# Output projection as seven half-size products, with half of the transposes under the last one

## The chip, the core and the metric

The kernel runs on one core of a Trainium2 chip. The time is what the device needs for one execution, in microseconds (us); lower is better. Work is done by TensorE (PE in the profile; its weight loads are PEld), VectorE (DVE), ScalarE (ACT), GpSimd (POOL) and by DMA transfers, which are issued from the queues of SyncE (SP), ScalarE and GpSimd. Each engine runs its own instructions in order and waits at semaphores for the others.

## The reference

One decoder block with x of 512 x 2048 (sequence S = 512, width D = 2048), in float32:

```python
h = rms_norm(x, norm1_g)
z = h @ w_in
o_rw = rwkv7_mix(token_shift(z[..., :3520], rw_mu), ...)
o_att = swa_attention(q, k, v, q_norm_g, k_norm_g, attn_sinks)
p_rw = o_rw @ w_branch[:1024]
p_att = o_att @ w_branch[1024:]
x = x + (sigmoid(zg_rw) * p_rw + sigmoid(zg_att) * p_att) @ w_out
h2 = rms_norm(x, norm2_g)
u = h2 @ w_up
c = causal_conv3(u) + conv_b
val, gate = split(c)
x = x + (silu(gate) * val) @ w_down
```

w_in is 2048 x 9152, w_out 2048 x 2048, w_up 2048 x 11264 (D_FF = 5632, twice), w_down 5632 x 2048.

## The kernel before, in words

Every product of float32 data is made of three matmuls: each operand is rounded to a reduced format (`hi`, on ScalarE) and the remainder is kept too (`lo`, on VectorE); hi x hi, lo x hi and hi x lo are added up in PSUM. A large product is therefore bound by its matmuls and fed by loads and splits.

The work runs in five stages.

- *First stage*, to about 1291 us. x is normalised and transposed, z is computed in 72 tiles of 128 columns, and attention, RWKV heads and gates are computed between them. `load_w` (L228 and following) loads 256 KB of weights into one of four `raw` buffers on SP's queue and splits it into `whi` and `wlo`. Each third call also runs one job of `sums_along`: a copy of 512 KB from DRAM to DRAM on SP's queue (L219) and an adding DMA of the same size on GpSimd's queue (L220). The 88 jobs make four sums of quarters of w_down, s1 to s4, for 11 blocks. The stage ends with the two branch outputs, o_at and o_rw, loaded back from DRAM and split.
- *Branch product*, L778 to L791, to about 1466 us. For each of 16 tiles m of 128 output columns, both halves of w_branch are multiplied (768 matmuls of 128 x 512), the gates are applied, and the merged tile is split into `mhi` and `mlo`, in SBUF (L790, L791).
- *Output projection*, L803 to L821, to about 1640 us. For four blocks of 512 columns, 16 tiles k and four row tiles, three matmuls each: 768 matmuls of 128 x 512. w_out comes through `load_w`, 64 loads of 256 KB. After each column block the sum is added to x1 (L818), squared for the norm (L820) and stored to `x1_d` (L821, GpSimd's queue).
- *Up projection*, to about 2573 us. x1 is normalised (a reduction L823, the small operations L187 to L194, the scaling L829/L831) and transposed by 64 TensorE transposes (L980), which are evacuated by ScalarE and VectorE (L990, L988). The transposed x1 is kept as four quarters q11, q12, q21, q22 (rows of weights by halves of the sequence). Then w_up is applied in 44 blocks, each as seven products of half size in place of eight, P1, P2, P7, P6, P5, Q4, P3, with 24 matmuls x 7 of 128 x 256 in a block (L899). Seven right-hand factors are made from the quarters and split (L994, L995): b11, b21, b22 are quarters, t1 = q11 - q12, t3 = q22 - q12, t2 = -t1 - q22 and t4 = -t2 - q21 are differences (L1049, L1050, L1056, L1057). Weights of a block are split on L885/L886. A list `steps` near L998 gives the order of products of neighbouring blocks; loads are issued from `queue`.
- *Down projection*, L1108 to the end. Also seven half-size products, each over 11 chunks; a chunk loads 256 KB of the right factor from DRAM (`h_d`, L1113), splits it (L1115, L1116), loads two weights or sums of 512 KB (L1119), splits them (L1121, L1122), and runs 24 matmuls of 128 x 512 (L1129). A product has 264 matmuls. The seven factors of h are made by VectorE in the up projection and written to DRAM by ScalarE's queue.

The seven-product form multiplies a 2 x 2 arrangement of blocks by seven block products, not eight. What it needs beside them are sums of weight quarters (s1 to s4 in DRAM) and differences of the right-hand quarters.

SBUF and PSUM come from pools; a tile that takes the place of an earlier one waits for the last reader of that place. Instructions on SP's queue run in order, so that a load that waits holds up all loads behind it. The planner that turns the program into five queues keeps the data's order and otherwise may move an instruction of one engine ahead of another; `pin` keeps some in program order.

Of the kernel before, what the change touches and what calls it, by code (L numbers as in the profile page):

```python
# [18 lines left out]
P = 128  # L19
# [115 lines left out]
def block_kernel(ctx: ExitStack, tc: tile.TileContext, d: Dims, a: dict, out: bass.AP):  # L135
# [11 lines left out]
    NB = NF // 4  # L147
    DH = d.D // 2
    h_d = [dram.tile([7, P, 2, S // 2], F32, name=f"h_d{j}") for j in range(NB)]
    sum_d = {n: [dram.tile([2, P, DH], F32, name=f"{n}_d{j}") for j in range(NB)] for n in ("s1", "s2", "s3", "s4")}  # L150

# [50 lines left out]
    def quarter(i, j, c):  # L202
        return a["w_dn"][i, j, 2 * c : 2 * c + 2]

    jobs = []
    for kinds in (
        (("s1", (1, 0), (1, 1)), ("s3", (0, 0), (1, 0))),
        (("s2", "s1", (0, 0)),),
        (("s4", "s2", (0, 1)),),
    ):  # L210
        jobs += [(k, c, q) for c in range(NB) for q in range(2) for k in kinds]
    pin = tc.keep_in_program_order

    def sums_along():

        if jobs:
            (n, first, second), c, q = jobs.pop(0)
            at = lambda src: (sum_d[src][c] if isinstance(src, str) else quarter(*src, c))[q]
            pin(sync.dma_start(sum_d[n][c][q], at(first), max_dma_last_dim=4096))  # L219
            pool.dma_start(sum_d[n][c][q], at(second), accum_op=ALU.add, max_dma_last_dim=4096)  # L220
# [7 lines left out]
    def load_w(src):  # L228
# [9 lines left out]
        if wp["n"] % 3 == 0:  # L238
            sums_along()
# [35 lines left out]
    if True:  # L275
# [466 lines left out]
        ohi = by_k(big(xbp, "ohi", "h2"), NP + NQ)  # L742
        olo = by_k(big(xbp, "olo", "l2"), NP + NQ)
        tbs = ExitStack()
        tb = tbs.enter_context(tc.tile_pool(name="tb", bufs=2, reuse_waits="tile"))
        srcs = []
        for nm, src, n in (("a", o_at_d, NQ), ("r", o_rw_d, NP)):
            at = 0 if nm == "r" else NP
            hi, lo = ohi[:, at : at + n], olo[:, at : at + n]
            for i in range(n):  # L750
                o = tb.tile([P, 2, S], F32, name="oin", tag="gin")[:, 0]
                act.dma_start(o, src[i * P : (i + 1) * P])
                split(hi[:, i], lo[:, i], o)
                if i % 2:
                    emit_gate()
            srcs.insert(0, (hi, lo, n))
        while gates:
            emit_gate()
    pa.close()
# [5 lines left out]
    wbc = ExitStack()  # L765
    open_weights(wbc, 4, 4)
    mhi = by_k(big(big1, "mhi", "h1"))
    mlo = by_k(big(big1, "mlo", "l1"))
    with ExitStack() as pbb:
        accp = pbb.enter_context(tc.tile_pool(name="accB", bufs=4, space=PSUM, reuse_waits="tile"))  # L770
        XC = NT * d.D // NK
        for m in range(NK):
            g = tb.tile([P, 2, S], F32, name="gin", tag="gin")
            for i in range(2):
                act.dma_start(g[:, i], gate_d[(i * NK + m) * P : (i * NK + m + 1) * P])
            r0 = 0
            for i, (hi, lo, n) in enumerate(srcs):
                acc = accp.tile([P, S], F32, name="acc", tag="acc")  # L778
                wb = a["w_b"][m].rearrange("p (k c) -> p k c", c=P)[:, r0 : r0 + n]
                project(acc, wb, hi, lo)  # L780
                if i == 0:
                    w = min(XC, d.D)
                    for e in range(m * XC, (m + 1) * XC, w):
                        t, c0 = divmod(e, d.D)
                        with tc.issue_after(wp["last"].ins):
                            sync.dma_start(x1[:, t, c0 : c0 + w], xd[t * P : (t + 1) * P, c0 : c0 + w])
                r0 += n
                dve.scalar_tensor_tensor(g[:, i], g[:, i], 1.0, acc, op0=ALU.add, op1=ALU.mult)
            dve.tensor_tensor(g[:, 0], g[:, 0], g[:, 1], op=ALU.add)
            act.activation(mhi[:, m], g[:, 0], AF.Copy, scale=0.5)  # L790
            dve.scalar_tensor_tensor(mlo[:, m], g[:, 0], 0.5, mhi[:, m].bitcast(F32), op0=ALU.mult, op1=ALU.subtract)  # L791
    tbs.close()
    xbs.close()


    KH = NK // 2
    TH = S // 2
    pc = ExitStack()
    tcp = pc.enter_context(tc.tile_pool(name="tcp", bufs=1, reuse_waits="tile"))
    cps = ExitStack()  # L800
    accp = cps.enter_context(tc.tile_pool(name="accC", bufs=8, space=PSUM, reuse_waits="tile"))
    CW = min(S, d.D)
    NCC = d.D // CW  # L803
    ssp = tcp.tile([P, NT, NCC], F32, name="ssp")
    for cc in range(NCC):
        cs = slice(cc * CW, (cc + 1) * CW)
        accs = [accp.tile([P, S], F32, name="acc", tag="acc") for _ in range(NT)]
        for k in range(NK):
            whi, wlo = load_w(a["w_out"][k * P : (k + 1) * P, cc * CW : (cc + 1) * CW].rearrange("(k p) c -> p k c", p=P))
            whi, wlo = whi[:, 0], wlo[:, 0]  # L810
            for t in range(NT):
# [36 lines left out]
    def raw_tile(nm="raw", n=6):  # L848
        return rwp.tile([P, WC], F32, name=nm, tag=nm, bufs=n)
# [366 lines left out]
```

## Time and profile before

| | |
|---|---|
| median of 3 runs | 3008.12 us (3006.22 to 3010.33) |
| profiled execution, its own time | 3003.21 us |
| its span | 3001.4 us |
| matmuls and transposes on TensorE | 18890 |
| busy: TensorE / VectorE / ScalarE / GpSimd | 2911.7 / 1904.8 / 1292.7 / 172.8 us |
| mean granted TensorE clock | 0.99 |

The profile is of one execution. Its busy times say how long each engine worked; the windows view cuts the span into stretches and gives the same per stretch, with the granted TensorE clock (1.00 is full) and the share of the 16 DMA engines in use. A row of the groups view reads: line, engine, operation, output <- inputs, shape, count | busy us, mean ns of one | idle time of that engine before them, and what ended it. A matmul's own duration there is longer than the distance between two matmuls, since they overlap; the pace is read from a long run of them in the chain of waits (start, length, what, count). A row of the timeline is start, length, engine, line, operation, and in brackets the idle time before it and what ended it.

### The profile page before, as it was taken

What the parts mean: (1) busy time and instruction counts of PE and PEld (TensorE: products, weight loads), DVE (VectorE), ACT (ScalarE), POOL (GpSimd) and SP (SyncE); (2) the same over time, 40 slices, a digit from 0 to 9 for tenths busy, and PEclk for the clock granted to TensorE, in tenths of its full rate; (3) what the DMA queues carried; (4) which work ended last, traced back from release to release, by engine and by line L of the source; (5) the groups of instructions that cost most, each with busy time, mean ns of one, the idle gap of its engine ahead of it and who ended that gap; (6) DMA issues with size and microseconds to landing.
All of it is one profiled execution on the core that took longest, in us unless ns stands there. A gap on an engine that the chain in (4) does not pass through costs nothing.

```text
span 3001.4 us, 48098 instructions
## 1 busy us (share of the span) xinstructions
PE 2911.7 (97%) x18890; PEld 2486.0 (83%) x18890; DVE 1904.8 (63%) x3183; ACT 1292.7 (43%) x2129; POOL 172.8 (6%) x224
## 2 busy tenths in 40 slices
PE   6899999999999999999999799999999999999999
PEld 5677777777777777788887799999999999888887
DVE  4456566666666766434333877777777787665555
ACT  4234344344334434422232545555555555444444
POOL 0000100000000000000000000000000000000000
PEclk9999999999999999999999999999999999999999
DMA  7654756656656656645444577778777777777775
GB/s 208 172 137 121 192 125 171 157 130 168 159 137 161 162 139 162 207 140 169 126 126 120 153 188 203 201 207 208 208 206 207 205 201 206 289 239 245 255 256 190
DMA packets 210582, 544.44 MB, mean 181 GB/s; under 512 B 23009, under 2 KB 43185, under 8 KB 209329
## 3 DMA queue, kind: packets, MB, share of 16 engines
q1 hardware_dynamic: 143136, 385.00, 42.3%
q0 software_dynamic: 28416, 104.87, 18.4%
q10 hardware_dynamic: 38800, 51.48, 5.1%
q8 instruction: 148, 2.42, 0.3%
q14 instruction: 82, 0.66, 0.1%
HBM read 498.95 MB, written 133.54 MB: 211 GB/s over the span
## 4 chain that ended last, share of the span: by engine, by line
PE 88%; DVE 4%; DMA 3%; ACT 2%; issue 1%; ACTq 0%; DVEq 0%; SPq 0%
PE X L899 16%; PE acc L251 10%; PE acc L252 10%; PE acc L250 9%; PE Y L899 8%; PE X L1129 8%; PE Y L1129 6%; PE Z L899 4%; PE acc L815 2%; PE acc L816 2%; PE acc L814 2%; DMA rsb<-rsd 1%; DMA rsd<-rsT 1%; PE mi L428 1%; PE bulk L674 1%
## 5 line engine op out<-in xcount | busy, mean ns | idle before, releaser
L235 ACT ACTIVATE whi<-raw 128x512 fp32r<-128x512 f32 x416 | 261.6, 630 | 587.5 <-PE acc L251 376.1
L236 DVE TENSOR_TENSOR wlo<-raw,whi 128x512 fp32r<-128x512 f32 x416 | 285.5, 689 | 325.3 <-ACT whi L235 316.5
L250 PE MATMUL acc<-xhi,whi 128*128 128x512 f32 x1152 | 468.6, 407 | 4.6 <-ACT whi L235 2.7
L252 PE MATMUL acc<-xhi,wlo 128*128 128x512 f32 x1152 | 471.6, 409 | 0.6 <-DVE wlo L236 0.5
L251 PE MATMUL acc<-xlo,whi 128*128 128x512 f32 x1152 | 469.4, 408 | 0.0
L1122 DVE TENSOR_TENSOR wlo<-raw,whi 128x1024 fp32r<-128x1024 f32 x154 | 188.4, 1225 | 153.9 <-ACT whi L1121 152.4
L899 PE MATMUL Y<-t,whi 128*128 128x256 f32 x1408 | 259.7, 285 | 11.3 <-ACT whi L885 6.7
L899 PE MATMUL X<-t,whi 128*128 128x256 f32 x1408 | 259.5, 285 | 5.0 <-ACT u L909 5.0
L886 DVE TENSOR_TENSOR wlo<-raw,whi 128x1024 fp32r<-128x1024 f32 x176 | 215.2, 1223 | 73.1 <-ACT whi L885 72.8
L899 PE MATMUL X<-b,whi 128*128 128x256 f32 x1408 | 258.0, 283 | 2.5 <-DVE b L995 1.6
L250 PEld LDWEIGHTS acc<-xhi,whi 128*128 128x128 f32 x1152 | 219.1, 190 | 46.9 <-issue 3.7
L252 PEld LDWEIGHTS acc<-xhi,wlo 128*128 128x128 f32 x1152 | 218.9, 190 | 43.3 <-issue 2.9
L251 PEld LDWEIGHTS acc<-xlo,whi 128*128 128x128 f32 x1152 | 219.3, 190 | 42.2 <-issue 1.2
L1121 ACT ACTIVATE whi<-raw 128x1024 fp32r<-128x1024 f32 x154 | 163.0, 1060 | 204.6 <-PE X L1129 102.9
L885 ACT ACTIVATE whi<-a 128x1024 fp32r<-128x1024 f32 x132 | 139.4, 1056 | 216.4 <-DVE a L880 210.1
L899 PEld LDWEIGHTS Y<-t,whi 128*128 128x128 f32 x1408 | 221.2, 193 | 12.2 <-ACT whi L885 6.9
L899 PEld LDWEIGHTS X<-t,whi 128*128 128x128 f32 x1408 | 221.4, 194 | 5.2 <-ACT u L909 5.2
L899 PEld LDWEIGHTS X<-b,whi 128*128 128x128 f32 x1408 | 219.8, 192 | 3.0 <-DVE b L995 1.8
L886 DVE TENSOR_TENSOR wlo<-a,whi 128x1024 fp32r<-128x1024 f32 x132 | 161.8, 1226 | 75.4 <-ACT whi L885 74.7
L899 PE MATMUL X<-t,wlo 128*128 128x256 f32 x704 | 200.6, 285 | 0.5 <-DVE wlo L886 0.5
L899 PE MATMUL Y<-t,wlo 128*128 128x256 f32 x704 | 200.2, 284 | 0.6 <-DVE wlo L886 0.6
L899 PE MATMUL X<-b,wlo 128*128 128x256 f32 x704 | 199.4, 283 | 1.1 <-DVE wlo L886 1.1
(326 smaller groups left out, 6037.5 us busy)
## 6 DMA issues: line engine op xcount, KB each, us to landing
raw<-in_w_up_dram SPq DMA_DIRECT2D x176, 512.0 KB
raw<-in_w_z_dram SPq DMA_DIRECT2D x288, 256.0 KB
s_d<-in_w_dn_dram POOLq DMA_DIRECT2D x88, 512.0 KB, 5.9
raw<-in_w_up_dram POOLq DMA_DIRECT2D x88, 512.0 KB, 9.2
raw<-s_d SPq DMA_DIRECT2D x88, 512.0 KB
raw<-in_w_dn_dram SPq DMA_DIRECT2D x66, 512.0 KB
s_d<-in_w_dn_dram SPq DMA_DIRECT2D x44, 512.0 KB
s_d<-s_d SPq DMA_DIRECT2D x44, 512.0 KB
```

The costliest lines, as they stand in the source:

```text
L235: act.activation(hi, raw, AF.Copy)
L236: dve.tensor_tensor(lo, raw, hi.bitcast(F32), op=ALU.subtract)
L250: pe.matmul(acc, whi[:, j], xhi[:, k], start=first, stop=False)
L251: pe.matmul(acc, whi[:, j], xlo[:, k], start=False, stop=False)
L252: pe.matmul(acc, wlo[:, j], xhi[:, k], start=False, stop=last)
L814: pe.matmul(dst, mhi[:, k, ts], whi, start=k == 0, stop=False)
L885: pin(act.activation(hi, t, AF.Copy))
L886: pin(dve.tensor_tensor(lo, t, hi.bitcast(F32), op=ALU.subtract))
L899: pin(pe.matmul(ps, l[:, k], r[:, k], start=start and k + i == 0, stop=last and i == 2, skip_group_check=True))
L1121: act.activation(whi, wr, AF.Copy)
L1122: dve.tensor_tensor(wlo, wr, whi.bitcast(F32), op=ALU.subtract)
L1129: pe.matmul(dst, l[:, q, ts], r[:, es], start=fst and j == 0, stop=lst and j == 2, skip_group_check=True)
```

## The change

The output projection takes the form of the down projection. w_out is arranged as quarters (`w_o`) like w_down, and both share the code: `PRODUCTS`, `steps_of` (one chunk: one 256 KB load of a right factor, its split, two loads of 512 KB, their splits, 24 matmuls) and `taken_out` (four additions into x). For w_out there are four chunks, 96 matmuls in a product, 672 in all. The sums s1 to s4 are made for w_out too: 120 jobs, those for w_out first, one at every second `load_w`.

The branch product takes the tiles m in pairs (attention half of m and m+1, then RWKV half of m and m+1). A merged pair is not split any more: VectorE makes t1, t3, t2, t4 from it, and ScalarE's queue stores three pieces (128, 256 and 512 KB) to `right_d["o"]` in DRAM. The RWKV half of the branch input is loaded by two DMAs of 1 MB on GpSimd's queue, and its split goes to the memory of the first stage's right-hand side. The weight tiles of the projection (`hlD`, `rawD`, `hhlC`) are opened where the branch product's right-hand side (`rhi`, `rlo`) and the other tiles of that stage were.

Under the last of the seven products the first half of the rows (row tiles 0 and 1) is normalised, transposed after two and after three of the four chunks (16 transposes each, by `transposed`), and split to b11 and b21. The other half is normalised and transposed between the first steps of the up projection. The accumulator Y of the up projection comes from its own pool, `upy`, and the first steps are reordered.

```diff
@@ sums
+    for w in ("o", "dn"):
+        for kinds in (
+            (("s1", (1, 0), (1, 1)), ("s3", (0, 0), (1, 0))),
+            (("s2", "s1", (0, 0)),),
+            (("s4", "s2", (0, 1)),),
+        ):
+            jobs += [(w, k, c, q) for c in range(NB[w]) for q in range(2) for k in kinds]
...
-        if wp["n"] % 3 == 0:
+        if wp["n"] % 2 == 0:
             sums_along()
@@ end of the first stage
+        for i in range(2):
+            pool.dma_start(rin[i], o_rw_d.rearrange("(i n p) s -> i p n s", i=2, p=P)[i])
         while gates:
             emit_gate()
+        rhi = by_k(big(big1, "rhi", "h1"), NP)
+        rlo = by_k(big(big1, "rlo", "l1"), NP)
+        for i in range(NP):
+            split(rhi[:, i], rlo[:, i], rin[2 * i // NP][:, i % (NP // 2)])
@@ branch product
-            act.activation(mhi[:, m], g[:, 0], AF.Copy, scale=0.5)
-            dve.scalar_tensor_tensor(mlo[:, m], g[:, 0], 0.5, mhi[:, m].bitcast(F32), op0=ALU.mult, op1=ALU.subtract)
+                if m % 2:
+                    tq = mp.tile([P, 4, TH], F32, name="tq", tag="tq")
+                    factors(tq, *mt, 0)
+                    factors(tq, *mt, 1)
+                    store_factors("o", m // 2, *mt, tq)
@@ output projection
-        for k in range(NK):
-            whi, wlo = load_w(a["w_out"][k * P : (k + 1) * P, cc * CW : (cc + 1) * CW].rearrange("(k p) c -> p k c", p=P))
...
+    def steps_of(w, i, acc, c, pl):
+
+        nm, start, src, right, _ = PRODUCTS[i]
+        hr = pl.tile([P, 2, TH], F32, name="hraw", tag="hraw")
+        sync.dma_start(hr, right_d[w][c][RIGHT_AT[right]])
+        hhi, hlo = (pl.tile([P, 2, TH], F32R, name=f"h{e}", tag=f"h{e}") for e in ("hi", "lo"))
+        act.activation(hhi, hr, AF.Copy)
+        dve.tensor_tensor(hlo, hr, hhi.bitcast(F32), op=ALU.subtract)
+        for q in range(2):
+            wr = raw_tile()
+            sync.dma_start(wr, quarter(w, src, c)[q])
+            whi, wlo = (hlp.tile([P, WC], F32R, name=f"w{e}", tag=f"w{e}") for e in ("hi", "lo"))
+            act.activation(whi, wr, AF.Copy)
+            dve.tensor_tensor(wlo, wr, whi.bitcast(F32), op=ALU.subtract)
...
+    def row_done(i, t, cc, cs):
+        sq = hp.tile([P, S], F32, name="sqc", tag="sqc", bufs=2)
+        act.activation(sq, x1[:, t, cs], AF.Square, accum_out=ssp[:, t, cc : cc + 1])
+        (act if i == 6 else pool).dma_start(x1_d[t * P : (t + 1) * P, cs], x1[:, t, cs])
...
+            if last:
+                yx.close()
+                tps = tpx.enter_context(tc.tile_pool(name="tpD", bufs=4, space=PSUM, side="right", reuse_waits="tile"))
+                normalise(0)
+            for c in range(NB["o"]):
+                steps_of("o", i, acc[nm], c, hp)
+                if last and c == NB["o"] - 3:
+                    transposed(tps, 0, 0, q11)
+                    split_q("b11", q11)
+                if last and c == NB["o"] - 2:
+                    transposed(tps, 1, 0, q21)
+                    split_q("b21", q21)
+            taken_out(i, acc[nm], x1, 0.5, row_done)
@@ first steps of the up projection
-    transposed(0, (q11, q12))
-    split_q("b11", q11)
-    transposed(1, (q21, q22))
...
+    run(0)
+    normalise(1)
+    run(1)
+    run(2)
+    transposed(tps, 0, 1, q12)
+    dve.tensor_tensor(q11, q11, q12, op=ALU.subtract)
+    run(3)
+    transposed(tps, 1, 1, q22)
...
+    dve.tensor_tensor(q12, q22, q12, op=ALU.subtract)
+    split_q("t3", q12)
+    run(4)
+    split_q("t1", q11)
+    dve.scalar_tensor_tensor(q11, q11, -1.0, q22, op0=ALU.mult, op1=ALU.subtract)
+    run(5)
+    split_q("t2", q11)
```

395 lines of the change are left out of this document (187 added, 208 removed).

## The prediction

> **What bounds the kernel now.** I read the page first: the busy times, the slices, and the chain of work that ended last.
>
> ```profile
> span 3001.4 us, 48098 instructions
> PE 2911.7 (97%) x18890; PEld 2486.0 (83%) x18890; DVE 1904.8 (63%) x3183; ACT 1292.7 (43%) x2129; POOL 172.8 (6%) x224
> PE   6899999999999999999999799999999999999999
> DMA  7654756656656656645444577778777777777775
> ...
> PE 88%; DVE 4%; DMA 3%; ACT 2%; issue 1%; ACTq 0%; DVEq 0%; SPq 0%
> ```
>
> TensorE is busy in 97% of the span and carries 88% of the chain, so the time is the number of matmuls times their pace, plus the places where TensorE waits. The slices show one such place after the start, a 7 in the 23rd slice, about 1650 us. The windows by stage say which stage that is (columns: window, its length, busy time of PE, PEld, DVE, ACT, POOL, granted clock, DMA share, GB/s):
>
> ```profile
> 0.00:100.00 100.00, 71.97 (x317) 56.94 (x317) 42.69 (x121) 38.28 (x70) 6.05 (x11) 0.93 0.75 211
> 900.00:1100.00 200.00, 198.34 (x1487) 151.02 (x1486) 134.76 (x297) 85.29 (x173) 12.62 (x16) 1.00 0.60 150
> 1291.00:1466.00 175.00, 175.00 (x774) 144.95 (x773) 80.55 (x124) 49.69 (x79) 0.00 (x0) 1.00 0.56 161
> 1466.00:1640.00 174.00, 174.00 (x769) 144.15 (x768) 52.84 (x79) 47.35 (x89) 7.07 (x13) 1.00 0.40 106
> 1640.00:1707.00 67.00, 47.76 (x330) 44.92 (x329) 57.00 (x68) 37.01 (x48) 7.40 (x11) 0.85 0.64 173
> 1707.00:2573.00 866.00, 856.55 (x7105) 855.14 (x7104) 675.99 (x809) 440.71 (x598) 71.87 (x82) 1.00 0.77 202
> 2573.00:3001.00 428.00, 423.05 (x1877) 349.63 (x1875) 254.98 (x267) 203.72 (x233) 2.17 (x4) 1.00 0.75 250
> ```
>
> The branch product (1291 to 1466) and the output projection (1466 to 1640) have no idle time at all. The seam from the projection to the up projection (1640 to 1707) has 19 us idle at a clock of 0.85. The other stages lose little.
>
> **What the matmuls that go are worth.** Groups of matmuls and the chain give the pace:
>
> ```profile
> L814 PE MATMUL acc<-whi,mhi 128*128 128x512 f32 x256 | 99.6, 389 | 0.0
> ...
> 2637.70 59.84 PE Y L1129 x264
> ```
>
> The projection is three such groups of 256, 768 matmuls; seven products of 4 chunks x 2 x 2 x 2 x 3 = 96 make 672. The chain's piece from the down projection is the same product form, 264 matmuls in 59.84 us, 0.2267 us each and without a gap. So the 96 that go are worth 96 x 0.2267 = 21.8 us. That form needs 8 weight loads of 512 KB and 4 of 256 KB for 96 matmuls, what the down projection needs too, where 250 GB/s were moved while TensorE stayed busy. I therefore cost the loads at nothing inside the projection; DMA and the splits below hide behind the matmuls.
>
> ```profile
> L1121 ACT ACTIVATE whi<-raw 128x1024 fp32r<-128x1024 f32 x154 | 163.0, 1060 | 204.6 <-PE X L1129 102.9
> L1122 DVE TENSOR_TENSOR wlo<-raw,whi 128x1024 fp32r<-128x1024 f32 x154 | 188.4, 1225 | 153.9 <-ACT whi L1121 152.4
> L1116 DVE TENSOR_TENSOR hlo<-hraw,hhi 128x512 fp32r<-128x512 f32 x77 | 52.7, 685 | 13.0 <-ACT hhi L1115 13.0
> L788 DVE SCALAR_TENSOR_TENSOR gin<-gin,acc 128x512 f32<-128x512 f32 x32 | 22.0, 688 | 49.8 <-PE acc L252 49.8
> ```
>
> Per product VectorE does 8 x 1.23 + 4 x 0.69 and four additions of 0.69, 15.3 us under 21.8 us of matmuls; without that cover they would cost themselves. In the branch product the split of the merged rows goes and factors and their stores come. VectorE was busy 80.6 of 175 us there; also nothing. Ahead of it, the eight splits of the RWKV half now wait for the last matmul of the first stage, whose memory they take: 8 x 0.69 = 5.5 us under the attention half's 48 matmuls of 0.2267, 10.9 us, for which weights are loaded already; nothing, or 5.5 without them.
>
> **Seam one, branch product to projection, is new.** Before, nothing waited there. Now the weight tiles of the projection lie in memory that the branch product's right-hand side has just left, so SP's first weight load waits for the last matmul of the branch product. SP's queue takes loads in order: everything behind it waits too. After that matmul come issue, landing, ScalarE's rounding, VectorE's remainder. The nearest rows are those at 1640 us, where SP also loads after a stage:
>
> ```profile
> 1640.49 0.33 SPq L870 DMA_DIRECT2D a<-in_w_up_dram  x1
> ...
> 1701.89 6.37 DMA a<-in_w_up_dram
> ...
> raw<-in_w_up_dram POOLq DMA_DIRECT2D x88, 512.0 KB, 9.2
> x_d<-x POOLq DMA_DIRECT2D x16, 256.0 KB, 3.8
> ```
>
> A 512 KB landing is between the 3.8 of a half-size transfer and 9.2 of a POOL load in a busy queue; I take the 6.4 of the load on SP's queue in the chain, since up to three 256 KB factor loads are ahead of ours. With 1.06 for the first rounding TensorE is idle 0.3 + 6.4 + 1.1 = 7.8 us; the third matmul wants the remainder, most of whose 1.2 us passes under two slow matmuls: 0.5 more, 8.3. VectorE's last merge and factors, some 2.6 us, pass under the landing. An idle stretch of that kind costs again through the clock, as the seam at 1675 us shows:
>
> ```profile
> 1675.04 0.58 PE L899 MATMUL Y<-t,whi 128*128 128x256 f32 x1 [6.66 <-ACT whi L885]
> ...
> 1675.04:1681.42 6.38, 4.95 (x19) 4.36 (x20) 6.34 (x5) 0.41 (x2) 0.00 (x0) 0.50 0.28 82
> 1794.75:1800.90 6.15, 5.96 (x26) 5.66 (x27) 4.95 (x6) 2.60 (x4) 0.00 (x0) 0.50 0.31 91
> ```
>
> After 6.7 us of idle time the granted clock was 0.50 for 6.4 us, and after another idle time for 6.2 us, so half of that, 3.2 us, is lost. Seam one: 8.3 + 3.2 = 11.5 us, between 5.7 + 3.2 = 8.9 with 3.8 and 11.1 + 3.2 = 14.3 with 9.2. Below nothing there is no room, since no idle time was there before.
>
> The Trainium skill, "TensorE: Matmul & The Clock Gate", Part 1 on the HAM clock gate, gives a re-warming of about 3.4 us at half rate after an idle window, which would cost 1.7 and not 3.2 us. By it the seam is 10.0 and the whole sum 1.5 us lower. The trace's two rows of over 6 us at 0.50 do not agree, and the sum goes by them.
>
> **The transposes under the last product.** Thirty-two of 64 transposes move from seam two to the last product:
>
> ```profile
> 1645.43 6.36 PE L980 MATMUL ps_t<-ident,x 128*128 128x128 f32 x32 [4.97 <-DVE x L831]
> 1652.81 3.71 PE L980 MATMUL ps_t<-ident,x 128*128 128x128 f32 x32 [1.02 <-DVE x L988]
> 1642.03 0.17 DVE L823 TENSOR_REDUCE ss<-ssp 128x4 f32<-128x16 f32 x1 [0.85 <-ACT sqc L820]
> ...
> 1644.42 0.16 DVE L194 SCALAR_TENSOR_TENSOR rq<-rq,rq 128x4 f32<-128x4 f32 x1
> 1644.62 2.74 DVE L831 TENSOR_SCALAR x<-x,rq 128x1024 f32<-128x1024 f32 x4
> ```
>
> At the full clock 32 take 3.7 us, and they stand between matmuls: +3.5. Their input needs four VectorE additions (2.8), squares, the chain from 1642.03 to 1644.6 with four splits between its steps on VectorE, and two scalings of 0.76 that also wait for the stores of x1: some 10 to 12 us after the product begins, while TensorE comes to them after two of four chunks, 48 x 0.2267 = 10.9 us. 0 to 2 us of wait; I take 1. Together +4.5.
>
> **Seam two, projection to up projection.** Before, the first eleven steps of the up projection and the 64 transposes run from the last matmul of the projection to here:
>
> ```profile
> 1640.07 0.39 PE L816 MATMUL acc<-wlo,mhi 128*128 128x512 f32 x1
> ...
> 1707.12 0.40 PE L899 MATMUL X<-t,whi 128*128 128x256 f32 x2
> ...
> 1639.18 1.41 ACT sqc L820 x4
> ...
> 1688.82 2.87 PE X L899 x24
> ...
> 1665.35 2.28 DVE L1049 TENSOR_TENSOR x<-x 128x2048 f32<-128x2048 f32 x1
> 1688.76 2.29 DVE L995 TENSOR_TENSOR t<-x,t 128x2048 fp32r<-128x2048 f32 x1
> ```
>
> From 1640.3 to 1707.1 are 66.8 us. Of them 11 x 24 matmuls of 0.12 (2.87 us for 24 in the chain) are 31.7 and the transposes some 7 at the full clock; 28 are stalls. With the change three steps can run at once, on the factors that were split under the last product. But the first weight's rounding stands behind four squares (1.41 for two with their accumulator reads, so 2.8) and the stores on ScalarE, and the remainder stands behind the second normalisation's small operations: first full pace at about +7.7 us. Three steps of 2.9 and the transposes bring it to +24. The next factor then needs, on VectorE alone and in a row, a difference, a remainder, evacuations, two differences and two more remainders, six operations of 2.28 and small ones: first ready at about +35. That is 11 idle us at the place where 6.7 were before, with the half clock behind it. From there the steps run, and the eleventh ends between +60 and +68. VectorE's chain, the old bound of the seam, still is its bound; only its beginning is earlier. Against 66.8 the term is -3, from -12 (the chain starts under the last product's end) to +8 (each VectorE step queued behind a weight's remainder).
>
> **The sums.** 88 sums become 120, and come every second weight load, no longer every third:
>
> ```profile
> q0 software_dynamic: 28416, 104.87, 18.4%
> q1 hardware_dynamic: 143136, 385.00, 42.3%
> L220 POOL DMA_DIRECT2D s_d<-in_w_dn_dram x88 | 72.0, 818 | 999.3 <-DMA s_d<-in_w_dn_dram 496.7 <-DMA s_d<-s_d 492.2 <-issue 10.4
> L252 PE MATMUL acc<-xhi,wlo 128*128 128x512 f32 x1152 | 471.6, 409 | 0.6 <-DVE wlo L236 0.5
> ```
>
> From the two queues 0.52 MB takes 0.184 x 3001 x 0.52 / 104.87 = 2.7 us of all engines when accumulated and 0.423 x 3001 x 0.52 / 385 = 1.7 when copied, 4.5 a sum; two 256 KB weights take 1.7. That is 6.2 us for every 24 matmuls of 0.2267, 5.4 us, where only projections follow each other: DMA falls behind 0.8 us in each such pair, and four raw buffers hold that for a while. Over the stage the 32 more sums raise the share from 0.60 by 32 x 4.5 / 1291 = 0.11. TensorE hardly waited for weights there (0.6 us before L252). I take +1.5, between 0 and +15.
>
> **The sum.** -21.8 + 11.5 + 4.5 - 3 + 1.5 = -7.3 us. The profiled execution took 3003.2 us (span 3001.4 and 1.8 around it), 4.9 below the median of the runs, 3008.1. The terms are differences, so I set them against the median: 3000.8 us.
>
> **The rivals.** *The seams are well covered.* If the first weight lands in 3.8 us (8.9 for seam one), nothing waits in the last product (3.5) and seam two gains 9: -21.8 + 8.9 + 3.5 - 9 = -18.4, 2989.7. For it: a quiet DMA at seam one; against it: VectorE is busy 57 of 67 us in seam two already.
>
> *VectorE makes seam two longer.* If each of its eight long operations lets one more 1.2 us remainder pass ahead, the seam grows by 8 to 10, not shrinks: -21.8 + 11.5 + 4.5 + 9 + 1.5 = +4.7; it decides from about +4 on, where the change gains nothing measurable. With a landing of 9.2 (+2.8) it is +7.5, 3015.6. For it: 57 of 67 us busy; against: the first splits are done earlier.
>
> *DMA bounds the first stage.* If the sums outrun the buffers in the dense stretches of each of eight head pairs by 2.5 us, 20 in place of 1.5: +11.2, 3019.3, slower. It decides where the loss passes about 15. For it: 6.2 against 5.4; against: between those stretches the share is low, as the mean of 0.60 says.
>
> *The products do not run at their pace* since factors and sums arrive late through the whole projection: 1 us per chunk, 28 us, 3029. The down projection, gapless on the same traffic, speaks against it.
>
> **How the numbers follow.** Forecast 0.42 (own range 2995 to 3007), covered seams 0.27, longer seam two 0.14, DMA in the first stage 0.13, pace 0.04. What a measurement can tell from no change is about 0.2%, 6 us: below 3002.1 faster, above 3014.1 slower. The forecast's case gives 0.25 to faster and 0.17 to same; covered seams 0.27 to faster; the longer seam splits into 0.05 same and 0.09 slower; the last two are slower. Faster 0.52, same 0.22, slower 0.26. The range 2984 to 3018 leaves out the far side of the last two and what lies beyond the covered seams.
>
> **What would show it.** In the changed profile: 672 matmuls in the projection at 0.2267 with gaps only at the transposes; a gap of about 8 us before its first matmul, released by the rounding of a weight, and then a clock of 0.50; a wait of 0 to 2 us at the first transposes; 60 to 68 us from the last projection matmul to the end of the eleventh step, with a gap near 11 us ended by the t3 factor's split; no new waits for weights in the first 1291 us. The prediction is wrong if seam one shows no gap, or if the first stage grows by over 5 us.

## The result, and the profile after

| | before | changed |
|---|---|---|
| median of 20 runs each, us | 3007.93 (2996.91 to 3011.46) | 3014.20 (3004.49 to 3027.93) |
| ratio to before, 95% interval | | 1.0024 (1.0013 to 1.0035) |
| span of the profiled execution, us | 3001.4 | 3003.2 |

The change makes the kernel slower, by 0.24%. 7.3 us less had been forecast; the measured difference of the medians is +6.3. The page of the changed kernel:

```profile
span 3003.2 us, 48149 instructions
PE 2895.8 (96%) x18794; PEld 2470.4 (82%) x18794; DVE 1955.3 (65%) x3243; ACT 1319.0 (44%) x2135; POOL 197.4 (7%) x254
PE   6899999999999999999999799999999999999999
DMA  8856867668768763647678477778777777877775
...
PE 84%; DMA 6%; DVE 5%; ACT 2%; issue 1%; ACTq 0%; DVEq 0%; SPq 0%
```

TensorE has 96 instructions and 16 us of work less, and yet the span is longer. The share of the chain that belongs to DMA has gone from 3% to 6%: TensorE gave work up and waits for transfers in its place. Where, the windows say (window, length, busy time of PE, PEld, DVE, ACT, POOL, granted clock, DMA share, GB/s), cut at the stage borders of the changed kernel:

```profile
900.00:1100.00 200.00, 194.97 (x1433) 149.42 (x1432) 130.27 (x292) 81.84 (x165) 19.91 (x25) 1.00 0.77 197
1306.10:1481.80 175.70, 175.70 (x769) 144.02 (x767) 87.72 (x146) 44.52 (x72) 0.00 (x0) 1.00 0.63 189
1481.80:1645.00 163.20, 158.03 (x705) 130.39 (x704) 110.12 (x137) 89.29 (x119) 8.94 (x15) 0.98 0.83 276
1645.00:1711.70 66.70, 43.67 (x297) 42.21 (x297) 50.27 (x57) 31.66 (x39) 3.19 (x6) 0.80 0.41 102
1711.70:2578.60 866.90, 859.72 (x7130) 858.82 (x7129) 678.49 (x814) 443.19 (x602) 70.55 (x82) 0.99 0.77 203
```

In the first of these windows TensorE idles 5.0 of 200 us, before 1.7; that is the first stage, in its middle. Where the stage ends is read from the last of its matmuls, in the view of one source line (count: shortest/median/longest ns, first and last start). Before, and after:

```profile
L252 PE MATMUL acc<-xhi,wlo x1152: 387/389/796, 35.1 to 1291.9; 128*128 128x512 f32 x192
```

```profile
L256 PE MATMUL acc<-xhi,wlo x1152: 387/389/796, 35.1 to 1305.8; 128*128 128x512 f32 x192
```

So the stages of the two profiled executions compare like this (us):

| stage | before | after | difference | forecast |
|---|---|---|---|---|
| first stage, to its last matmul | 1291.9 | 1305.8 | +13.9 | +1.5 |
| branch product | 174.1 | 175.8 | +1.7 | 0 |
| seam one and output projection | 174.1 | 163.2 | -10.9 | -5.8 |
| seam two, to the end of the eleventh step | 66.8 | 66.6 | -0.2 | -3 |
| the rest, to the last matmul | 1289.2 | 1286.8 | -2.5 | 0 |

The sum is +2.0. The medians differ by 4 us more; the runs of the changed kernel spread over 23 us, and the profiled execution lies at their low end. The stage that lost most is the one in which nothing but the sums and the ends was changed.

What TensorE waited for in the first stage, before (what waited <- what came last: us in total, times, longest):

```profile
PE scp L394 <- DVE qn L357: 13.5, 6, 4.1
PE mi L374 <- ACT vf L371: 6.8, 2, 4.3
PE acc L252 <- DVE wlo L236: 0.5, 1, 0.5
```

and after:

```profile
PE scp L398 <- DVE qn L361: 14.7, 5, 4.0
PE mi L378 <- ACT vf L375: 8.8, 2, 5.5
PE acc L256 <- DVE wlo L240: 8.0, 4, 2.8
PE psU L689 <- DVE G L687: 2.4, 3, 0.9
```

The new wait is for `wlo`, the remainder of a weight, which VectorE makes. But VectorE is not busy then, as its timeline and TensorE's show at the longest of the four (start, length, operation; in brackets the idle time ahead of it and what ended it):

```profile
1015.66 0.27 DVE L334 COPY rsT<-bulk 8x128 f32<-8x128 f32 x1
1022.76 0.69 DVE L240 TENSOR_TENSOR wlo<-raw,whi 128x512 fp32r<-128x512 f32 x1 [6.83 <-ACT whi L239]
1029.05 0.69 DVE L726 TENSOR_TENSOR yc<-yc,rsb 128x512 f32<-128x512 f32 x1 [5.59 <-DMA rsb<-rsd]
1029.78 0.55 DVE L727 TENSOR_SCALAR yc<-yc,par 128x512 f32<-128x512 f32 x1
1030.24 0.68 DVE L240 TENSOR_TENSOR wlo<-raw,whi 128x512 fp32r<-128x512 f32 x1
```

```profile
1030.97 0.50 PE L256 MATMUL acc<-xhi,wlo 128*128 128x512 f32 x1 [2.81 <-DVE wlo L240]
```

VectorE stands for 5.6 us at L726, which needs `rsb`. The row norms of a head pair go to DRAM in a 4 KB store (`rsd<-rsT`) and come back spread over the partitions in two loads of 128 KB (`rsb<-rsd`). From `rsT` at 1015.7 to the use of `rsb` at 1029.0 are 13.4 us. The next `wlo` is behind L726 in VectorE's order, so TensorE runs out of weights although the weights are there. All four waits for `wlo` have a pause of VectorE for `rsb` ahead of them, three at L726 and the first at L542, which needs an `rsb` too. In total VectorE waits at L726 even less than before:

```profile
DVE yc L726 <- DMA rsb<-rsd: 19.2, 8, 5.6
```

Before, it was 23.0 us in eight waits, but none was longer than 3.7. The four waits for `wlo` explain 7.5 of the 13.9 us. That it is the sums that lengthen some of these round trips is so far a guess; the experiments test it.

### The profile page after: what moved, and what is told of

Its sections match the earlier page's. It is cut to its first block, busy times and chain, and to the rows that moved or that the text cites. A ratio compares the mean times of both kernels' runs of the same rounds, so it can differ in the third digit from the quotient of the medians.

```text
span 3003.2 us, 48149 instructions
## 1 busy us (share of the span) xinstructions
PE 2895.8 (96%) x18794; PEld 2470.4 (82%) x18794; DVE 1955.3 (65%) x3243; ACT 1319.0 (44%) x2135; POOL 197.4 (7%) x254
## 4 chain that ended last, share of the span: by engine, by line
PE 84%; DMA 6%; DVE 5%; ACT 2%; issue 1%; ACTq 0%; DVEq 0%; SPq 0%
PE X L1023 16%; PE X L875 11%; PE acc L255 9%; PE acc L256 9%; PE acc L254 9%; PE Y L1023 8%; PE Y L875 8%; PE Z L1023 4%; DMA rsb<-rsd 3%; DMA rsd<-rsT 2%; PE mi L432 1%; PE bulk L678 1%; PE bulk L616 1%; PE bulk L655 1%; DMA raw<-in_w_z_dram 1%
## 5 line engine op out<-in xcount | busy, mean ns | idle before, releaser
L239 ACT ACTIVATE whi<-raw 128x512 fp32r<-128x512 f32 x352 | 220.6, 630 | 527.7 <-PE acc L255 403.7
L240 DVE TENSOR_TENSOR wlo<-raw,whi 128x512 fp32r<-128x512 f32 x352 | 240.7, 688 | 237.5 <-ACT whi L239 234.7
L868 DVE TENSOR_TENSOR wlo<-raw,whi 128x1024 fp32r<-128x1024 f32 x210 | 257.1, 1225 | 206.9 <-ACT whi L867 206.6
L867 ACT ACTIVATE whi<-raw 128x1024 fp32r<-128x1024 f32 x210 | 222.6, 1061 | 286.5 <-PE X L875 146.6
L1008 DVE TENSOR_TENSOR wlo<-raw,whi 128x1024 fp32r<-128x1024 f32 x176 | 215.1, 1222 | 79.3 <-ACT whi L1007 78.8
L256 PEld LDWEIGHTS acc<-xhi,wlo 128*128 128x128 f32 x1152 | 218.9, 190 | 51.6 <-DVE wlo L240 10.5
L1023 PEld LDWEIGHTS Y<-t,whi 128*128 128x128 f32 x1408 | 224.0, 196 | 19.2 <-ACT t L941 9.1
```

The source lines that it names most:

```text
L239: act.activation(hi, raw, AF.Copy)
L240: dve.tensor_tensor(lo, raw, hi.bitcast(F32), op=ALU.subtract)
L256: pe.matmul(acc, wlo[:, j], xhi[:, k], start=False, stop=last)
L867: act.activation(whi, wr, AF.Copy)
L868: dve.tensor_tensor(wlo, wr, whi.bitcast(F32), op=ALU.subtract)
L1008: pin(dve.tensor_tensor(lo, t, hi.bitcast(F32), op=ALU.subtract))
```

## The experiments

All ratios are to the kernel before on the same chip, with 95% intervals. Each run's expectation stands as it was recorded ahead of it. In the first two that name it, e1 and e4, "the last z matmul" is one near the end of the stage, behind its long waits (1240 before, 1257 after); from e7 on it is the last of the stage (1292 and 1306).

**Are the sums the cause?** e1 takes w_out's sums out again, e2 adds 32 sums to the kernel before, e3 only moves that kernel's own sums closer together.

In e1, on the changed kernel, the projection reads a raw quarter where it read a sum:

```diff
-    for w in ("o", "dn"):
+    for w in ("dn",):
...
-        if wp["n"] % 2 == 0:
+        if wp["n"] % 3 == 0:
```

e2 and e3, on the kernel before, share the second edit; the first is e2's alone:

```diff
+    jobs = [((None, (1, 0), (1, 1)), c, q) for c in range(16) for q in range(2)]
...
-        if wp["n"] % 3 == 0:
+        if wp["n"] % 2 == 0:
```

> The changed kernel with the 32 sums of w_out left out and the 88 of w_down again at every third load; the four products of the projection that use a sum read a raw quarter of w_out instead, same size and shape. Theory crowding (the 16 us that the first stage lost come from its sums' transfers): the last z matmul is back from 1257 to within 3 us of 1240, and the time is 13 to 17 us below the changed kernel, 2997 to 3001, a ratio to before of 0.996 to 0.998. Rival (the first stage lost its time to the other edits at its end, the two 1 MB loads on GpSimd's queue and the late splits): it stays near 1257 and the ratio at 1.002.

Measured: 2990.93, ratio 0.9950 (0.9938 to 0.9962), last matmul of the stage at 1289.9.

> The kernel before with 32 more sums (their results are not used), 120 in all, one at every second load; nothing else is changed. Theory crowding: its first stage ends 14 to 17 us later, the time is 3021 to 3025, ratio 1.0045 to 1.0060, with a wider scatter of the runs as in the changed kernel. Rival (the other edits): ratio 1.000 to 1.001.

Measured: 3029.65, ratio 1.0082 (1.0067 to 1.0097), last matmul of the stage at 1314.2.

> The kernel before with its own 88 sums at every second load, so that they end after 176 of 288 loads. Theory density (what counts is how closely the sums follow each other): it loses as the changed kernel did over the same loads, about 10 us by the 176th load, and keeps that to the end, ratio 1.003. Rival amount (what counts is the number of bytes over the whole stage): what is lost early comes back in the freed last third, ratio within 0.001 of 1.

Measured: 3023.29, ratio 1.0054 (1.0038 to 1.0069), last matmul of the stage at 1317.1.

The sums are the cause: without them the change gains 16 us against before, and with them alone the kernel before loses 22. All three effects are larger than expected; by their ratios, e1 and the changed kernel are 0.0074 x 3007 = 22 us apart. e3 moves no byte more than the kernel before and loses 16 us, so it isn't the amount, and what is lost early does not come back.

**Bursts or rate?** e4 halves each transfer and makes twice as many.

```diff
+            es = slice(e * P // 2, (e + 1) * P // 2)
+            dst = sum_d[w][n][c][q][es]
...
-        if wp["n"] % 2 == 0:
-            sums_along()
+        sums_along()
```

> The changed kernel with every sum in two transfers of 256 KB, one at every load: the same bytes at the same mean rate in smaller bursts. Theory burst (a small transfer waits behind one whole 512 KB piece): the first stage gets back about half, the last z matmul at 1249, time 3006, ratio to before 0.999 to 1.000. Rival rate (the share of the DMA engines decides): last z matmul at 1255 to 1262, ratio 1.002 to 1.004.

Measured: 3008.91, ratio 1.0002 (0.9991 to 1.0013). The median is just outside what smaller bursts should give; the profiled execution doesn't show a gain, with the stage's last matmul at 1312.2, later than in the changed kernel's profile (which was of one of its fastest executions). Of the 22 us some 6 or 7 may be the size of a piece (0.0022 x 3007); since the two intervals touch, that isn't shown.

**Spread sums, and seam one.** e5 spreads the sums over three stages; e6 lets the projection's first loads run under the branch product; e7 does both, and e9 profiles the same program a second time. `sums_late` adds up the sum that was copied at its last call and copies the next. The edit of e5:

```diff
-        if wp["n"] % 2 == 0:
+        if wp["n"] % (3 if wp["n"] <= 288 else 9) == 0:
             sums_along()
...
+        if n == "P3" and f > 3 and f % 2:
+            sums_late()
```

The edit of e6:

```diff
-        rhi = by_k(big(big1, "rhi", "h1"), NP)
-        rlo = by_k(big(big1, "rlo", "l1"), NP)
+        rhl = by_k(big(big1, "rhl", "l1"))
+        rhi, rlo = rhl[:, :NP], rhl[:, NP:]
...
+        eng = pool if w == "o" and pair == NK // 2 - 1 else act
...
+        hold = pin if w == "o" and i == 0 else free
+        hold(sync.dma_start(hr, right_d[w][c][RIGHT_AT[right]]))
...
+        if w == "o" and i == 0 and c == 0:
+            mms.sort(key=lambda m: m[0])
```

> The changed kernel with the same 120 sums, spread: one at every third load of the first stage (96), every ninth load of the branch product (7), and the last 17, which only the down projection reads, one at every second block of the up projection from the sixth on. Theory density: the first stage ends where it did before (last z matmul within 3 us of before's), and the time is near the run without w_out's sums, 2991 plus 2 to 6 for the sums that now run beside the branch product and the up projection: 2993 to 2998, ratio 0.995 to 0.997. Rival (the same bytes cost the same wherever they run, since the up projection's loads fill 0.77 of the DMA engines): the loss moves to the up projection, ratio 1.000 to 1.003.

Measured: 2997.66, ratio 0.9974 (0.9962 to 0.9986), last matmul of the first stage at 1300.4. Faster than both kernels, but by the ratio less than expected. The rival is wrong about the place: the up projection took the 17 sums at a DMA share of 0.85 and was not longer, 867.8 us from the eleventh step to its end, against 866.9 in the changed kernel. It is the first stage that did not come back fully.

> The changed kernel with its sums as they are, but the first weights of the projection free to load under the branch product: the RWKV half of the branch input lies in another part of the same memory, the raw tiles in the part that is free, SP's first loads keep the program's order, the last pair's factors are stored from GpSimd's queue so that ScalarE rounds ahead, and in the first chunk the four matmuls that need no VectorE result come first. Theory seam (5.3 us idle before the projection and 2 us of half clock come from the first weight's wait for the last branch matmul): the idle time falls to about 3.5 us in two pieces, 3 to 5 us less in all, ratio to before 1.0005 to 1.0015. Rival (VectorE's last merge and factors hold the seam anyway): less than 1 us, ratio 1.002.

Measured: 3008.23, ratio 1.0010 (0.9995 to 1.0025). In the traces the branch product's end and the projection's end are 159.1 us apart, 163.2 in the changed kernel: 4.1 us; seam two is 1.3 us longer in this trace. The seam in the changed kernel, in the chain (start, length, what):

```profile
1482.04 3.97 DMA raw<-in_w_o_dram
...
1486.03 1.06 ACT whi L867
```

in TensorE's timeline:

```profile
1487.14 0.80 PE L875 MATMUL X<-whi,hhi 128*128 128x512 f32 x1 [5.13 <-ACT whi L867]
```

and in two windows behind it:

```profile
1487.10:1490.50 3.40, 3.32 (x7) 2.21 (x8) 1.54 (x2) 1.11 (x2) 0.00 (x0) 0.50 1.01 336
1490.50:1494.00 3.50, 3.50 (x16) 2.83 (x16) 2.92 (x3) 2.07 (x2) 0.00 (x0) 0.96 1.04 413
```

The first weight's load and its rounding fill the gap, and 3.4 us at half the clock follow. In e6, TensorE's timeline:

```profile
1484.55 1.21 PE L884 MATMUL X<-whi,hlo 128*128 128x512 f32 x4 [2.43 <-DVE hlo L867]
```

The load is gone from the path, VectorE's work is what is left, and the full clock stays: the granted clock is 1.00 from here to 1488. Three of the next matmuls follow after 0.32 to 0.34 us, the others at 0.23 to 0.24.

> Both edits together, spread sums and the prefetch at the seam. If the two are independent the gains add up: 3 to 5 us below the run with spread sums alone, 2989 to 2994, ratio 0.9935 to 0.9955. If the seam's loss is VectorE's, it equals that run within 1 us.

Measured: 2996.29, ratio 0.9970 (0.9958 to 0.9982), last matmul of the first stage at 1294.8. Only 1.4 us below e5; the intervals overlap, so that run alone doesn't tell whether the gains add.

> The run with spread sums and the prefetch once more on the same chip, for a second profile: the end of its first stage shows how much of that differs from execution to execution. In the profile above the last z matmul came at 1295; within 4 us of it is expected.

Measured: one run of 2999.84, last matmul at 1300.8, 6 us from e7's profile, and outside the 4 us expected. With the same program the stage's end differs by 6 us from execution to execution, more than the seam's gain.

**A miss that changed the theory.** e8 puts still fewer sums into the first stage.

```diff
-        if wp["n"] % (3 if wp["n"] <= 288 else 9) == 0:
+        if wp["n"] % (4 if wp["n"] <= 288 else 9) == 0:
...
-        if n == "P3" and f > 3 and f % 2:
+        if n == "P3" and f >= 2:
```

> The kernel with spread sums and the prefetch, spread further: one sum at every fourth load of the first stage (72), 7 beside the branch product, and 41 in the up projection, one a block. Theory density: the first stage ends another 3 to 8 us earlier than with every third load, and the up projection, whose DMA share rises from 0.77 by 41 x 4.5 / 866 = 0.21 to 0.98, begins to wait for weights; if it holds, 2989 to 2993, ratio 0.9945 to 0.996; if its loads fall behind, the up projection grows by 5 to 20 us and the ratio is 0.999 to 1.004.

Measured: 3007.53, ratio 1.0004 (0.9992 to 1.0016). It looks like the rival, and isn't: the up projection from its eleventh step is 868.3 us long, as before (869.1). The first stage ends at 1313.6, with a DMA share in its middle that is below the 0.62 of the kernel before:

```profile
300.00:1240.00 940.00, 922.01 (x6512) 702.04 (x6512) 604.61 (x1335) 380.20 (x767) 52.38 (x71) 1.00 0.54 135
```

Its timelines of SP, ScalarE and GpSimd's queues and of VectorE and TensorE around one of the waits:

```profile
911.74 0.51 SPq L223 DMA_DIRECT2D s_dn<-in_w_dn_dram  x1
...
912.78 0.29 ACTq L336 DMA_DIRECT2D rsd<-rsT  x1
...
917.16 0.80 POOL L224 DMA_DIRECT2D s_dn<-in_w_dn_dram  x1 [13.48 <-DMA s_dn<-in_w_dn_dram]
...
917.54 1.10 ACTq L340 DMA_DIRECT2D rsb<-rsd  x2
...
924.49 0.69 DVE L726 TENSOR_TENSOR yc<-yc,rsb 128x512 f32<-128x512 f32 x1 [4.44 <-DMA rsb<-rsd]
926.42 0.50 PE L256 MATMUL acc<-xhi,wlo 128*128 128x512 f32 x1 [1.44 <-DVE wlo L240]
```

The copy goes out 1.0 us ahead of the small store, the adding transfer 0.4 us ahead of the loads back; the round trip lasts 11.7 us (912.8 to 924.5). A tile of z takes four loads, so a sum at every fourth load always comes at the end of a tile, and the same meeting returns in each pair of heads. e10, on the changed kernel, and e11, on e8, move the sums and change nothing else; e12 is e11 with 1 for the 2.

```diff
-        if wp["n"] % 2 == 0:
+        if wp["n"] % 2 == 1:
```

```diff
-        if wp["n"] % (4 if wp["n"] <= 288 else 9) == 0:
+        if wp["n"] % 4 == 2 if wp["n"] <= 288 else wp["n"] % 9 == 0:
```

> The changed kernel with its 120 sums after every first and third load of a tile of four, not after every second and fourth: the same number, bytes and density, moved by one load. In the thin run fewer sums cost more, which no theory of density gives; there a copy was issued 1.1 us ahead of the small store (rsd) whose loads back (rsb) VectorE waits for, in each pair of heads. Theory meeting (a sum costs where it runs into that round trip, and with every second or fourth load it always comes at the same place): the first stage ends 8 to 17 us earlier, last z matmul at 1290 to 1297, 2997 to 3006, ratio 0.997 to 1.000. Theory density: no change, ratio 1.002 to 1.004.

Measured: 3018.51, ratio 1.0044 (1.0028 to 1.0060), last matmul at 1316.2.

> The thin run with its sums after the second load of each tile, not after the fourth. Theory meeting: it gets back the 13 to 18 us that its first stage lost against the run with spread sums and the prefetch, last z matmul at 1291 to 1297, 2990 to 2995, ratio 0.995 to 0.9965. Theory density or amount: as the thin run, ratio 1.000.

Measured: 2980.68, ratio 0.9922 (0.9910 to 0.9933), last matmul at 1283.8.

> The thin run with its sums after the first load of each tile. Theory meeting: between the two, since the copy's adding transfer, 5 us behind it, may still meet the round trip: last z matmul at 1291 to 1310; if it equals the run after the second load, the place of the copy alone decides. Theory density or amount: as the thin run, ratio 1.000.

Measured: 2984.03, ratio 0.9933 (0.9920 to 0.9946), last matmul at 1283.9.

Two loads' difference in place is worth 27 us between the medians of e8 and e11 (25 by their ratios), with the same sums, the same bytes and about the same share. The window of e11:

```profile
300.00:1240.00 940.00, 923.70 (x6485) 704.13 (x6484) 607.91 (x1333) 381.67 (x759) 49.48 (x63) 0.99 0.55 143
```

its timelines at the same step of the kernel as above:

```profile
882.07 1.10 ACTq L340 DMA_DIRECT2D rsb<-rsd  x2
885.52 0.69 DVE L726 TENSOR_TENSOR yc<-yc,rsb 128x512 f32<-128x512 f32 x1 [0.95 <-DMA rsb<-rsd]
```

and VectorE's waits for `rsb` at L726 from 300 to 1240:

```profile
DVE yc L726 <- DMA rsb<-rsd: 12.1, 8, 5.6
```

From the loads back to their use are 3.5 us, where e8 needs 7.0. The last row's counterpart in e8:

```profile
DVE yc L726 <- DMA rsb<-rsd: 30.9, 7, 4.5
```

In the second to seventh pair of heads the round trip, from the store's issue to its use, takes 10.7 to 11.7 us in e8, 6.4 to 7.4 in e11 and 6.7 to 7.6 in e12. In e12 the copy goes out 0.2 us behind the store, in e8 1.0 to 1.3 us ahead of it. By the condition recorded for e12, which ends its stage where e11 does, the place of the copy decides at this rate; the adding transfer moves with it, so the two are not told apart.

But L726 is the smaller part of the 27 us. Each trace has 1152 matmuls of hi x lo in z; the table says when some of them start, in the runs as the difference to the kernel before (us). The first L726 comes just behind the 384th.

| | 192nd | 384th | 1024th | 1152nd |
|---|---|---|---|---|
| before, start | 255.8 | 465.1 | 1186.7 | 1291.9 |
| changed kernel | +6.3 | +5.5 | +16.9 | +13.9 |
| e2 | +8.8 | +10.5 | +21.4 | +22.3 |
| e8 | +10.2 | +14.8 | +23.1 | +21.7 |
| e10 | +12.6 | +15.6 | +26.6 | +24.2 |
| e11 | -12.3 | -14.9 | -15.2 | -8.1 |
| e15 | -6.0 | -10.9 | -10.7 | -1.0 |

e11 is 29.7 us ahead of e8 before any L726 has run. The eight pairs add 8.6, and the stage's end takes about as much away. So most of it is decided in the attention heads, whose norms of k and q take the same round trip through DRAM, at L361. There TensorE itself waits for the result. Its row of waits for the norm of q up to 300 us, and the window, in e8 and then in e11:

```profile
PE scp L398 <- DVE qn L361: 18.5, 5, 4.5
0.00:300.00 300.00, 250.51 (x1233) 192.21 (x1234) 148.55 (x458) 106.87 (x271) 15.03 (x21) 0.93 0.53 139
```

```profile
PE scp L398 <- DVE qn L361: 9.0, 5, 3.0
0.00:300.00 300.00, 265.75 (x1373) 205.79 (x1374) 161.18 (x483) 117.47 (x298) 20.91 (x34) 0.97 0.56 151
```

These waits are 9.5 us apart; the rest of the 29.7 is not placed. In the changed kernel it is the other way about: 5.5 us are lost up to the 384th and 11.4 in the eight pairs, and 3.0 come back at the end.

But e10 shows that the place is not all: with two sums in every four loads it loses no less from the other place. The last three runs try that, and what the projection is worth by itself.

e13, on the changed kernel:

```diff
-        if wp["n"] % 2 == 0:
+        if wp["n"] % 4 in (1, 2):
```

e14 is the changed kernel with e11's sums and without e6's edits. e15, on the kernel before:

```diff
-        if wp["n"] % 3 == 0:
+        if wp["n"] % 4 == 2 and wp["n"] <= 288:
             sums_along()
...
+        if n == "P3" and f > 3 and f % 2:
+            sums_late()
```

> The changed kernel with its 120 sums after the first and the second load of each tile, two in every four loads as in the changed kernel, but none after the third or fourth. Theory place (only the sums after the last load of a tile meet the round trip): first stage as in the thin run after the second load, last z matmul at 1284 to 1292, time 2988 to 2998, ratio 0.994 to 0.9975. Theory density (two sums in every four loads leave no free time, wherever they are): last z matmul at 1304 to 1317, ratio 1.002 to 1.006.

Measured: 3006.63, ratio 1.0011 (0.9999 to 1.0023), last matmul at 1302.8: between the two theories, below the changed kernel in the median but with intervals that overlap.

> The changed kernel with the sparse sums of the thin run after the second load of each tile (72 in the first stage, 7 beside the branch product, 41 in the up projection) and without the prefetch at the seam. Theory sums (all that was lost is theirs): 2981 plus the seam's 4 us, 2983 to 2987, ratio 0.993 to 0.9945. If the gain of that run came from both edits together, more than 6 us above it.

Measured: 2987.22, ratio 0.9948 (0.9932 to 0.9963). 6.5 us above e11, or 8 by the ratios (the two ran on different chips), more than the 4.1 that the seam shows in the traces; the rest is not placed.

> The kernel before with its 88 sums placed likewise: 72 after the second load of each tile of the first stage, 16 in the up projection, one at every second block. Theory: its first stage too ends some 6 to 8 us earlier, as those of the two thin runs (1284 against 1292), 2997 to 3001, ratio 0.997 to 0.9985; the difference to e14, 12 to 16 us, is then what the seven products and their seams are worth. If the sums at every third load cost the kernel before nothing: ratio 1.000.

Measured: 3003.22, ratio 0.9996 (0.9986 to 1.0007). The kernel before gains nothing by it that can be told. In its trace the first stage is, matmul for matmul, 11 us ahead of the kernel before at 1221 us, more than the theory wants, and then loses 10 of them in the end of the stage:

```profile
PE acc L250 <- ACT whi L235: 10.7, 3, 6.6
```

There ScalarE, in order, waits for `oin`, the branch inputs, with roundings of weights behind it. e11 and e14 lose 7 us in the same stretch, so the ends differ by little. Another 5 us go in the up projection, 874.3 us from the eleventh step, where the kernel before takes 869.1 and e14 868.4; why is open. So the 16 us between e14 and e15 are not what the projection and its seams alone are worth.

## Why the prediction was wrong, point by point

- **The term that failed** is "I take +1.5, between 0 and +15" for the sums. In the profiled executions the stage took +13.9, and between the changed kernel and e1, by the ratios, lie 22. The step behind it compared the DMA engines' mean share and the four raw buffers with the pace of weights. That was beside the point: weights mostly did come in time. What came late were small stores and their loads back. The eight pairs cost 11.4 us of the profile's 13.9; about 6 of them are waits for `wlo`, where VectorE's order puts the weights' remainders behind the round trip. In the attention heads TensorE waits for the round trip itself. The kernel before had the row for the pairs among VectorE's waits in its first stage; the prediction left it out, and those waits cost TensorE next to nothing then:

```profile
DVE yc L722 <- DMA rsb<-rsd: 23.0, 8, 3.7
```

- The rival "DMA bounds the first stage", at 0.13, had the right sign, stage and size (20 us put down), but not the mechanism: with the sums at every fourth load DMA is far from full (0.54), and the stage still ended 22 us late. That its size fits is luck.
- **Seam one** was oversized: 11.5 forecast, 5.1 idle and half of 3.4 us at a clock of 0.50, 6.8 in all. The landing took 3.97 and not 6.37 us, near the lower bound of the term; the half clock lay over 3.4 us of matmuls and not 6.3. This is the figure of the Trainium skill, "TensorE: Matmul & The Clock Gate", Part 1, which the prediction set aside by two other rows; here the trace agrees with it. The mechanism (first weight behind the last branch matmul) is shown by e6.
- **The 96 matmuls and the transposes** came as forecast. The window from 1481.8 to 1645.0 is 672 x 0.2267 = 152.3, plus 6.8 for the seam and about 3.5 for the transposes: 162.6 of 163.2. The transposes had no wait ahead of them:

```profile
1630.63 1.91 PE L926 MATMUL ps_t<-ident,x 128*128 128x128 f32 x16
1637.86 1.91 PE L926 MATMUL ps_t<-ident,x 128*128 128x128 f32 x16
```

- **Seam two** gained nothing: -0.2 where -3 was taken (-12 to +8). The steps that can now run early do run, and TensorE waits longer further on:

```profile
1650.17 0.79 PE L1023 MATMUL X<-b,whi 128*128 128x256 f32 x2 [4.95 <-ACT whi L1007]
1678.79 0.58 PE L1023 MATMUL Y<-t,whi 128*128 128x256 f32 x1 [8.83 <-ACT t L941]
1700.75 0.80 PE L1023 MATMUL Y<-t,whi 128*128 128x256 f32 x2 [4.85 <-DVE u L1041]
```

  The first wait for the P1 weight, 4.95, was forecast at about 7.7 to full pace; the wait for t3's split, 8.83, at about 11. The third wait is new. By the windows TensorE is idle for 23.0 us of the seam, before for 19.2; the 32 transposes that went under the last product (3.7 us) made up for that.
- With the sums out of the way (e1) the change is worth -16 us in the medians. The forecast without its last term is -8.8, and the stages behind the first give -11.9 in the profiled executions (1.7 - 10.9 - 0.2 - 2.5); the 4 or 5 us between are not placed, and lie within what the first stage differs by from one execution to the next. e14, at -17, also has a first stage that is 6 us shorter than before's, which is the thinner sums' doing and not the products'.

## What to carry to other kernels

Before bulk transfers are added beside a stage, look for small round trips through DRAM on which an in-order engine waits, and for what is queued behind that wait or waits for it; the mean share of the DMA engines doesn't show them. Where background transfers are hung on a loop's counter, try the counter's phase as well as its rate: at one in four, two loads' difference was 27 us, and with a stride that divides the loop's own period the same meeting came back in every pair of heads. At two in four no place tried here was free of loss. And count, instruction for instruction, where the time went before settling on the wait that is easiest to see: here most of the 27 us lay ahead of it. Work that is only needed late (the sums for the down projection) can go to a later stage even at a high share: the up projection carried 41 of them, at 0.94 of the DMA engines, without becoming longer (868 us from the eleventh step in e8, e11, e12 and e14, 869.1 in the kernel before). It isn't always free: with 16 or 17 of them, one at every second block, it took 867.8 (e5), 870.4 (e9), 872.0 (e7) and 874.3 (e15).

The fastest version here, e11 (spread sums after the second load, and the prefetch), runs in 2980.68 us, 0.78% (0.67% to 0.90%) below the kernel before.

## What was not expected of the hardware

- The up projection at a DMA share of 0.94 in e11:

```profile
1700.00:2550.00 850.00, 840.32 (x6978) 839.53 (x6978) 663.11 (x798) 432.02 (x589) 104.22 (x121) 0.99 0.94 254
```

  From its eleventh step to its end are 868.2 us, against 869.1 in the kernel before at 0.77. So a share of 0.94 did not hurt this stage, where at 0.54 the first stage lost 22 us in e8.
- In the branch product of the changed kernel the matmuls are further apart at a full clock without any wait: 768 in 175.8 us, 0.2289 each, where the kernel before takes 174.1, 0.2267 each. All runs with the new branch product show it (1.7 us). What it comes from is open.
- After the idle time at seam one the matmuls ran at a clock of 0.50 for 3.4 us, after two others of 5 and 7 us in the kernel before for more than 6. The slow clock begins within the idle time, as windows of it show, seam one in the changed kernel and then the seam at 1675 us in the kernel before:

```profile
1484.00:1487.10 3.10, 0.00 (x0) 0.00 (x0) 0.68 (x2) 1.06 (x1) 0.00 (x0) 0.50 0.91 325
```

```profile
1671.20:1675.00 3.80, 0.00 (x0) 0.00 (x0) 3.80 (x3) 2.87 (x3) 0.00 (x0) 0.50 0.00 0
```

  In the trace's record of the clock the slow stretch lasts from 1484.0 to 1490.8 in the first case and from 1671.2 to 1681.4 in the second. What these two seams paid is what was left of it when the matmuls came back.
